# Seven columns of the second norm's modulation move from VectorE to GpSimd and ScalarE, inside the output projection's first half

## The chip, the cores and the metric

One NeuronCore of a Trainium2 chip runs the whole program. The metric is device time in microseconds (us) of one execution; before the change it is 1054.03 us, the median of 3 runs (1051.93 to 1054.62).

## The reference

One decoder layer for 256 tokens of width 2048, in float32. A conditioning vector c is turned into six vectors of 2048 numbers (shift, scale and gate for each of two sub-layers), by one product with a 2048 x 12288 matrix. What matters here is cut to these lines:

```python
c_act = jax.nn.silu(c)
mod = c_act @ w_mod[l] + b_mod[l]
sh1, sc1, g1, sh2, sc2, g2 = [m[:, None, :] for m in jnp.split(mod, 6, axis=-1)]
h = rmsnorm(x, attn_norm_g[l]) * (1.0 + sc1) + sh1
...                                   # input projection, two kinds of attention
mix = jnp.concatenate([o_a, o_b], axis=-1)
x = x + g1 * jnp.einsum('bsm,md->bsd', mix, w_out[l])
h = rmsnorm(x, mlp_norm_g[l]) * (1.0 + sc2) + sh2
u = jax.nn.relu(jnp.einsum('bsd,df->bsf', h, w_ff1[l]))
x = x + g2 * jnp.einsum('bsf,fd->bsd', u * u, w_ff2[l])
```

The second norm is the line with `sc2` and `sh2`: 16 blocks of 128 features each need one 128-wide column of `sc2` and one of `sh2`, 32 columns in all.

## The kernel before

Activations lie with features on the 128 partitions and the 256 tokens along the free axis; `x_sb` holds 16 such blocks. Large weights come in tiles of 128 x 2048 float32 (1 MB) by DMAs that SP issues. Weights of the two projections treated here are split into a high and a low part, 1024 columns at a time (`split`): ScalarE makes the high part (L191), VectorE subtracts it to get the low part (L192), and TensorE does three products for each 128 x 128 block (`mm3`, L197 to L199).

A modulation column (`mod_col`) is one 1 MB load (L161) and one VectorE instruction of 128 x 2048 that multiplies by the conditioning vector `c_bc`, sums along the row and adds the bias (L168), with a read of the accumulator behind it. The 32 columns of the second norm stand in a list, `modq`, in the order sc2, sh2, sc2, ...; `pump_mod(n)` takes the next n. Six are taken after the input projection (`NPRE`), behind the 16 columns of `g1`.

The output projection runs in two halves of the contraction. Half 0 takes the 8 heads' blocks of `mix[0]`, half 1 those of `mix[1]`. In each half, eight loads of `w_out` (dp = 0 to 7, L530) give two output tiles each (`out_tile`, d = 0 to 15): split, 24 matmuls, and a VectorE instruction that scales by `g1` and adds to `x_sb` (L536). The first two tiles of half 0 are put between the last units of attention; the other 14 follow it. In half 1 each tile's squares go into the second norm's sum (`SumSq`: ScalarE squares, GpSimd adds at L512), and `PB = (0, 1)` with `PBN = 8` takes one column of `modq` for each dp, eight in all. The other 18 are taken in the first part of the MLP's first product (the loop over kt after `pf`, called ff1a here, 48 matmuls for each kt): one for each kt from 1 on (`LEADK`), and more where the block kt itself would come without its pair. That makes two each at kt = 12, 13 and 14. `h2_tile(kt)` needs its two columns: GpSimd scales and multiplies (L693, L694), ScalarE adds the shift (L695), VectorE makes the low part (L696).

Buffers: weight tiles turn over three buffers (`NW`), columns over two (`NM`). The pool `at` holds attention's tiles and is closed at the beginning of half 1; in the room that it leaves stand the token-major tile `xt` and a pool `wide` with `WW = 4` further weight buffers and `WM = 2` further column buffers, until ff1a ends. Tile, the scheduling layer, sets each engine's order when the program is built, by the order of the source with some parts given priority, and puts in the waits; each engine's queue then runs in that order.

Of the kernel before, what the change touches and what calls it, by code (L numbers as in the profile page):

```python
# [9 lines left out]
F32 = mybir.dt.float32  # L10
F32R = mybir.dt.float32r
AF = mybir.ActivationFunctionType
ALU = mybir.AluOpType

P = 128
D = 2048
S = 256
KT = D // P
# [10 lines left out]
V_BMOD, V_GA, V_GM, V_GF, V_GQ, V_GKV = 0, 96, 112, 128, 144, 147  # L29
# [13 lines left out]
LEAD = 0  # L43
BORD = (1, 0)
BORD2 = (0, 1)
WW = 4
WM = 2
G2F = (1, 5)
G2E = (3, 4, 5, 6)
LEADK = (1, 1)  # L50
PBN = 8


@with_exitstack
def kernel(
# [21 lines left out]
    nc = tc.nc  # L77
    V, A, G, T = nc.vector, nc.scalar, nc.gpsimd, nc.tensor
# [9 lines left out]
    def bank(name):  # L88
        return ps.tile([P, 512], F32, tag="bank", name=name)

    def small(name, n=1, bufs=1):
        return keep.tile([P, n], F32, tag=name, name=name, bufs=bufs)
# [6 lines left out]
    vec = small("vec", 148)  # L99
# [18 lines left out]
    c_bc = keep.tile([P, D], F32, name="c_bc")  # L118
# [9 lines left out]
    b1 = small("b1", 32)  # L128
# [4 lines left out]
    wide = {}  # L133
# [171 lines left out]
    sc2, sh2 = {}, {}  # L305
    modq = [(p, i) for i in range(KT) for p in (4, 3)]

    def pump_mod(n):
        for _ in range(n):
            if modq:  # L310
                p, i = modq.pop(0)
                (sc2 if p == 4 else sh2)[i] = mod_col(p, i)
# [127 lines left out]
    def swa_values(u0, u1):  # L440

        u0.po.append(bank(f"po{u0.name}"))
        for kb in range(u0.b + 1):
            u0.value(kb)
            u1.value(kb)
        mix_out(u0.po[0], 4 * u0.half, u0.b)
# [79 lines left out]
    def out_tile(half, d):  # L526
        dp, d2 = divmod(d, 2)
        if d2 == 0:
            wo[half] = raw(f"wo{half}_{dp}")
            nc.sync.dma_start(wo[half], w_out[half, dp])  # L530
        wh, wl = split(wo[half], d2, f"wo{half}_{dp}")
        pd = bank(f"pd{half}_{d}")
        for k in range(8):
            o = k * P
            mm3(pd[:, 0:S], wh[:, o : o + P], wl[:, o : o + P], mix[half][:, k, :], k == 0, k == 7)
        V.scalar_tensor_tensor(out=x_sb[:, d, :], in0=pd[:, 0:S], scalar=g1[d], in1=x_sb[:, d, :],  # L536
                               op0=ALU.mult, op1=ALU.add)

    with tc.high_priority():
# [92 lines left out]
        for n, u in enumerate(units):  # L632
# [14 lines left out]
            elif n % 2:  # L647
                swa_values(units[n - 1], u)

    def to_tokens(dp):  # L650
        pt = bank(f"xt{dp}")
        for t in range(2):
            for i in range(2):
                T.transpose(out=pt[:, (2 * t + i) * P : (2 * t + i + 1) * P],
                            in_=x_sb[:, 2 * dp + i, t * P : (t + 1) * P], identity=ident)
        A.activation(out=xt[:, :, 2 * dp * P : (2 * dp + 2) * P], in_=pt.rearrange("p (t c) -> p t c", t=2),
                     func=AF.Copy)

    for half in range(2):
        if half:  # L660
            ap_stack.close()
            late = ctx.enter_context(tc.tile_pool(name="late", bufs=1))
            xt = late.tile([P, 2, D], F32, name="xt")
            wide_stack = ExitStack()
            wide.update(pool=wide_stack.enter_context(tc.tile_pool(name="wide", bufs=1)), w=WW, m=WM)
        for dp in range(8):
            for d2 in range(2):
                d = 2 * dp + d2
                if half or dp:
                    out_tile(half, d)  # L670
                if half:
                    ss2.add(d)
                if half == 0 or dp < PBN:
                    pump_mod((PA, PB)[half][d2])
            if half and dp:
                to_tokens(dp - 1)

    with tc.high_priority():
        r2 = ss2.rstd()
    to_tokens(7)  # L680


# [289 lines left out]
```

## Time and profile before

| | before |
|---|---|
| median of 3 runs | 1054.03 us |
| profiled execution | 1053.02 us |
| its span, first to last instruction | 1051.2 us |
| TensorE busy | 1008.8 us (96%) |
| VectorE busy | 723.2 us (69%) |
| ScalarE busy | 487.4 us (46%) |
| GpSimd busy | 101.2 us (10%) |
| mean DMA rate | 267 GB/s |

The profiled execution spends 1.8 us outside its span. The views are read by stretches of time: attention ends near 222 us, half 0 of the output projection ends near 262, half 1 near 310, and ff1a runs from 317 to about 418. The names PE, DVE, ACT, POOL and SP in the rows are TensorE, VectorE, ScalarE, GpSimd and the queue that issues the DMAs; the time from the start of one record to the start of the next is the rate at which an engine works, since records overlap a little.

### The profile page before, as it was taken

Reading aid. Unit: us, or ns where it says so; the run is one execution under the profiler, and the core shown is the slowest. Engines: PE = TensorE matmul, PEld = TensorE weight load, DVE = VectorE, ACT = ScalarE, POOL = GpSimd, SP = SyncE. Lnnn points to the kernel's source line nnn. Section 1 sums busy time; section 2 is a strip of 40 time slices with the busy share of each in tenths; the row PEclk is TensorE's granted clock in tenths of the full one; section 3 lists DMA queues with packets and bytes.
Section 4 is the critical chain, followed back from the end, with each engine's and each line's share of the span. In section 5 each row is a group of like instructions: output and inputs, shape, how many; then the busy total and the mean of one; then the engine's idle time right before and its main releaser. Section 6 shows DMA issues by size and latency. Waiting matters only on the chain.

```text
span 1051.2 us, 14181 instructions
## 1 busy us (share of the span) xinstructions
PE 1008.8 (96%) x5582; PEld 866.6 (82%) x5582; DVE 723.2 (69%) x923; ACT 487.4 (46%) x824; POOL 101.2 (10%) x78
## 2 busy tenths in 40 slices
PE   6999989999987998999999999999999999999996
PEld 5777766799977998888888888888888888888885
DVE  5676769999987887897774555545555566554673
ACT  2000087743553443884444665334566543455461
POOL 0000014000448325000000000000000000000110
PEclk9999999999998999999999999999999999999998
DMA  8999986889996875889887655555555555555551
GB/s 328 422 420 420 410 333 240 307 327 398 419 387 255 308 258 228 319 323 339 312 304 257 224 177 189 195 200 200 172 189 196 177 191 196 201 185 179 197 200 80
DMA packets 44259, 280.24 MB, mean 267 GB/s; under 512 B 6880, under 2 KB 9120, under 8 KB 13088
## 3 DMA queue, kind: packets, MB, share of 16 engines
q1 hardware_dynamic: 44192, 279.34, 71.1%
q8 instruction: 43, 0.70, 0.3%
q14 instruction: 24, 0.20, 0.1%
HBM read 277.19 MB, written 2.13 MB: 266 GB/s over the span
## 4 chain that ended last, share of the span: by engine, by line
PE 73%; DVE 10%; DMA 8%; ACT 4%; POOL 2%; issue 2%; SPq 0%; ACTq 0%; DVEq 0%; POOLq 0%
PE pu L203 17%; PE pd L814 11%; PE pd L812 11%; PE pd L813 11%; PE pu L204 9%; DMA wm<-in_w_mod 7%; DVE wm L168 5%; PE pj L271 5%; PE pf L199 2%; PE pf L198 2%; PE pf L197 2%; POOL xn L693 1%; DVE wo_lo L192 1%; DMA wo<-in_w_out 1%; ACT ssa L349 1%
## 5 line engine op out<-in xcount | busy, mean ns | idle before, releaser
L192 DVE TENSOR_TENSOR wf_lo<-wf,wf_hi 128x1024 fp32r<-128x1024 f32 x250 | 308.5, 1239 | 222.9 <-ACT wf_hi L191 222.3
L191 ACT ACTIVATE wf_hi<-wf 128x1024 fp32r<-128x1024 f32 x250 | 263.7, 1056 | 238.0 <-PE pd L814 169.1
L203 PE MATMUL pu<-h,wf_hi 128*128 128x512 f32 x768 | 270.2, 397 | 0.0
L204 PE MATMUL pu<-h,wf_lo 128*128 128x256 f32 x768 | 215.5, 281 | 0.0
L812 PE MATMUL pd<-wf_hi,u 128*128 128x512 f32 x488 | 189.9, 389 | 0.0
L814 PE MATMUL pd<-wf_hi,u 128*128 128x512 f32 x488 | 189.9, 389 | 0.0
L813 PE MATMUL pd<-wf_lo,u 128*128 128x512 f32 x488 | 189.9, 389 | 0.0
L203 PEld LDWEIGHTS pu<-h,wf_hi 128*128 128x128 f32 x768 | 144.1, 188 | 34.7
L168 DVE CUSTOM_DVE_ANT_0 wm<-wm,c_bc,vec 128x2048 f32<-128x2048 f32 x64 | 151.5, 2367 | 14.2 <-DMA wm<-in_w_mod 14.1
L204 PEld LDWEIGHTS pu<-h,wf_lo 128*128 128x128 f32 x768 | 145.1, 189 | 0.1
L271 PE MATMUL pj<-h,wi 128*128 128x256 f32 (+1 forms) x480 | 113.1, 392 | 7.8 <-ACT h L257 7.8
L271 PEld LDWEIGHTS pj<-h,wi 128*128 128x128 f32 (+1 forms) x480 | 89.0, 191 | 31.4 <-ACT h L257 12.7
L814 PEld LDWEIGHTS pd<-wf_hi,u 128*128 128x128 f32 x488 | 91.6, 188 | 19.0
L812 PEld LDWEIGHTS pd<-wf_hi,u 128*128 128x128 f32 x488 | 91.6, 188 | 19.0
L813 PEld LDWEIGHTS pd<-wf_lo,u 128*128 128x128 f32 x488 | 91.6, 188 | 19.0
L168 DVE CUSTOM_DVE_ANT_0 wm<-wm,c_bc,b 128x2048 f32<-128x2048 f32 x32 | 75.9, 2371 | 31.3 <-DMA wm<-in_w_mod 31.2
L199 PE MATMUL pf<-h,wf_lo 128*128 128x256 f32 x256 | 74.4, 294 | 5.9 <-DVE wf_lo L192 5.9
L197 PE MATMUL pf<-h,wf_hi 128*128 128x256 f32 x256 | 74.0, 293 | 6.1 <-ACT h L695 5.0
L197 PE MATMUL pd<-mix,wo_hi 128*128 128x256 f32 x256 | 73.9, 289 | 1.3 <-ACT wo_hi L191 1.3
L198 PE MATMUL pf<-h,wf_hi 128*128 128x256 f32 x256 | 74.4, 292 | 0.0
L199 PE MATMUL pd<-mix,wo_lo 128*128 128x256 f32 x256 | 72.5, 284 | 0.0
L198 PE MATMUL pd<-mix,wo_hi 128*128 128x256 f32 x256 | 72.5, 283 | 0.0
(195 smaller groups left out, 1095.1 us busy)
## 6 DMA issues: line engine op xcount, KB each, us to landing
wm<-in_w_mod SPq DMA_DIRECT2D x96, 1024.0 KB, 9.2
wf<-in_w_ff SPq DMA_DIRECT2D x64, 1024.0 KB, 4.8
wf<-in_w_ff1b SPq DMA_DIRECT2D x48, 1024.0 KB, 4.9
wo<-in_w_out SPq DMA_DIRECT2D x16, 1024.0 KB, 12.1
wf<-in_w_ff1a SPq DMA_DIRECT2D x16, 1024.0 KB, 8.5
wi<-in_w_in SPq DMA_DIRECT2D x15, 928.0 KB, 13.9
x_sb<-in_xT SPq DMA_DIRECT2D x4, 512.0 KB, 5.5
bias<-g_dr SPq DMA_DIRECT2D x2, 1024.0 KB, 12.5
```

The source lines that it names most:

```text
L168: V.tensor_tensor_reduce(out=t, in0=t, in1=c_bc, scale=1.0, scalar=init, op0=ALU.mult, op1=ALU.add, accum_out=col)
L191: A.activation(out=hi, in_=src, func=AF.Copy)
L192: V.tensor_tensor(out=lo, in0=src, in1=hi.bitcast(F32), op=ALU.subtract)
L197: T.matmul(out, lhsT=wh, rhs=a[:, 0:S], start=start, stop=False, **kw)
L198: T.matmul(out, lhsT=wh, rhs=a[:, S : 2 * S], start=False, stop=False, **kw)
L199: T.matmul(out, lhsT=wl, rhs=a[:, 0:S], start=False, stop=stop, **kw)
L203: T.matmul(out, lhsT=wh, rhs=a, start=start, stop=False)
L204: T.matmul(out[:, 0:S], lhsT=wl, rhs=a[:, 0:S], start=False, stop=stop)
L271: T.matmul(proj(j)[: e - j * P, :], lhsT=w[:, j * P : e], rhs=h, start=(kt == 0 and j % 2 == 0), stop=(kt == KT - 1), skip_group_check=True)
L812: T.matmul(pd[t], lhsT=uh, rhs=wh[:, o : o + 512], start=(f == 0), stop=False)
L813: T.matmul(pd[t], lhsT=uh, rhs=wl[:, o : o + 512], start=False, stop=False)
L814: T.matmul(pd[t], lhsT=ul, rhs=wh[:, o : o + 512], start=False, stop=(f == KT - 1))
```

## The change

`pool_mod` does one column without VectorE's long instruction: the load goes to a buffer of its own (tag `widep`, 2 buffers), GpSimd multiplies by `c_bc` in place (128 x 2048), ScalarE copies the result in place and sums it into a column, and VectorE adds the bias (128 x 1). It is called seven times, ahead of the two tiles of dp = 1 to 7 in half 0. For that, attention's pool is closed and `xt` and `wide` are opened at the beginning of half 0 instead of half 1. The further weight buffers go from 4 to 3 and the further column buffers from 2 to 1, which is the room of the two `widep` buffers. `PBN` goes from 8 to 4, so four columns are taken in half 1 instead of eight. By the same count 15 instead of 18 are left for ff1a: one for each kt from 1 to 15.

```diff
-WW = 4
-WM = 2
+WW = 3
+WM = 1
 G2F = (1, 5)
 G2E = (3, 4, 5, 6)
 LEADK = (1, 1)
-PBN = 8
+PBN = 4
...
+    def pool_mod():
+
+        p, i = modq.pop(0)
+        t = wide["pool"].tile([P, 2048], F32, tag="widep", name=f"wp{p}_{i}", bufs=2)
+        nc.sync.dma_start(t, w_mod[p * KT + i])
+        G.tensor_tensor(out=t, in0=t, in1=c_bc, op=ALU.mult)
+        col = small(f"mod{p}_{i}")
+        A.activation(out=t, in_=t, func=AF.Copy, accum_out=col)
+        init = b1[:, 16 + i : 17 + i] if p == 4 else vec[:, V_BMOD + p * KT + i : V_BMOD + p * KT + i + 1]
+        V.tensor_tensor(out=col, in0=col, in1=init, op=ALU.add)
+        (sc2 if p == 4 else sh2)[i] = col
+
...
     for half in range(2):
-        if half:
+        if half == 0:
             ap_stack.close()
             late = ctx.enter_context(tc.tile_pool(name="late", bufs=1))
             xt = late.tile([P, 2, D], F32, name="xt")
             wide_stack = ExitStack()
             wide.update(pool=wide_stack.enter_context(tc.tile_pool(name="wide", bufs=1)), w=WW, m=WM)
         for dp in range(8):
+            if half == 0 and dp:
+                pool_mod()
             for d2 in range(2):
```

## Rows read from the trace of the kernel before

**Rows 1.** Windows by stage: length, busy time (instructions) by engine, PE clock, DMA share, GB/s.
```profile
222.00:262.00 40.00, 38.70 (x315) 37.80 (x315) 38.00 (x46) 13.10 (x13) 0.00 (x0) 1.00 0.97 383
262.00:310.00 48.00, 47.04 (x391) 46.73 (x391) 45.66 (x49) 23.33 (x35) 22.98 (x14) 1.00 1.00 408
317.30:343.00 25.70, 22.25 (x146) 21.38 (x147) 18.65 (x22) 8.86 (x14) 20.12 (x14) 0.84 0.66 252
343.00:397.00 54.00, 54.00 (x452) 54.00 (x451) 47.46 (x48) 20.77 (x22) 19.03 (x10) 1.00 0.77 287
```

**Rows 2.** VectorE's groups from 222 to 310: count, busy us, mean ns, idle before.
```profile
L192 DVE TENSOR_TENSOR wo_lo<-wo,wo_hi 128x1024 fp32r<-128x1024 f32 x27 | 34.7, 1300 | 1.8 <-ACT wo_hi L191 1.6
L168 DVE CUSTOM_DVE_ANT_0 wm<-wm,c_bc,b 128x2048 f32<-128x2048 f32 x8 | 19.0, 2370 | 0.1
L536 DVE SCALAR_TENSOR_TENSOR x_sb<-pd,mod,x_sb 128x256 f32<-128x256 f32 x28 | 13.3, 476 | 1.9 <-PE pd L199 1.9
L168 DVE DVE_READ_ACCUMULATOR2_ANT mod<- 128x1 f32 x16 | 1.3, 79 | 0.0
```

**Rows 3.** Windows at the end of ff1a, and one from its middle (columns as in Rows 1).
```profile
397.00:403.00 6.00, 5.70 (x48) 5.50 (x47) 5.00 (x6) 2.41 (x3) 2.30 (x2) 1.00 0.98 399
403.00:409.00 6.00, 4.71 (x38) 4.30 (x36) 4.83 (x5) 2.40 (x3) 3.15 (x2) 1.00 0.91 381
409.00:415.00 6.00, 4.02 (x21) 4.02 (x22) 5.44 (x7) 0.00 (x0) 4.99 (x2) 0.72 0.01 4
349.00:355.00 6.00, 6.00 (x52) 6.00 (x51) 4.36 (x6) 2.71 (x4) 3.21 (x2) 1.00 0.91 358
```

**Rows 4.** GpSimd's two-input products, undisturbed, 256 and 512 wide: start, duration.
```profile
321.74 0.74 POOL L694 TENSOR_TENSOR xn<-xn,r_y 128x256 f32<-128x256 f32 x1
1021.86 1.29 POOL L848 TENSOR_TENSOR xt<-x_sb,gf_row 128x512 f32<-128x512 f32 x1 [18.48 <-DVE x_sb L846]
```

**Rows 5.** Timeline: GpSimd and VectorE at work at the same time.
```profile
978.14 3.52 POOL L848 TENSOR_TENSOR xt<-x_sb,gf_row 128x512 f32<-128x512 f32 x2 [563.08 <-DVE x_sb L846]
978.52 4.22 DVE L192 TENSOR_TENSOR wf_lo<-wf,wf_hi 128x1024 fp32r<-128x1024 f32 x2
...
999.84 3.53 POOL L848 TENSOR_TENSOR xt<-x_sb,gf_row 128x512 f32<-128x512 f32 x2 [18.18 <-DVE x_sb L846]
1002.15 1.25 DVE L852 TENSOR_TENSOR sbase<-ssum 128x2 f32<-128x2 f32 x1
...
303.98 2.19 POOL L512 TENSOR_TENSOR sqa<-sqa,sqr 128x256 f32<-128x256 f32 x1 [2.13 <-ACT sqr L510]
303.25 2.34 DVE L168 CUSTOM_DVE_ANT_0 wm<-wm,c_bc,vec 128x2048 f32<-128x2048 f32 x1
305.51 0.47 DVE L536 SCALAR_TENSOR_TENSOR x_sb<-pd,mod,x_sb 128x256 f32<-128x256 f32 x1
```

**Rows 6.** Groups of ScalarE: a copy of 1024, a square of 256, an accumulator read.
```profile
L191 ACT ACTIVATE wo_hi<-wo 128x1024 fp32r<-128x1024 f32 x32 | 33.5, 1053 | 34.0 <-PE pd L198 22.1 <-DMA wo<-in_w_out 11.9
L510 ACT ACTIVATE sqr<-x_sb 128x256 f32<-128x256 f32 x15 | 6.3, 417 | 13.7 <-DVE x_sb L536 13.7
L847 ACT ACTIVATION_READ_ACCUMULATOR pd<-x_sb 128x1 f32 x8 | 1.5, 186 | 0.0
```

**Rows 7.** Timeline of a load, attention's last matmul, a split; then landing times.
```profile
201.58 0.33 SPq L530 DMA_DIRECT2D wo<-in_w_out  x1
...
222.30 0.38 PE L486 MATMUL pob<-pTb,vB 128*128 128x128 f32 x2
225.22 1.06 ACT L191 ACTIVATE wo_hi<-wo 128x1024 fp32r<-128x1024 f32 x1 [1.90 <-PE pd L198]
...
DMA to landing us min/median/max: 5.9/12.1/18.7
```

**Rows 8.** What TensorE waited for from 195 to 310, the two projection rows.
```profile
PE pd L197 <- ACT wo_hi L191: 1.3, 3, 0.5
PE pr L515 <- POOL sqa L512: 1.0, 1, 1.0
```

**Rows 9.** Window of the highest DMA rate in the output projection (columns as in Rows 1).
```profile
250.00:275.00 25.00, 24.18 (x199) 23.68 (x198) 22.53 (x28) 11.37 (x14) 4.45 (x3) 1.00 1.01 423
```

## The prediction

> **What bounds the kernel now.** I read the windows by stage first. In half 0 of the output projection after attention (222 to 262 us) and in half 1 (262 to 310) TensorE is busy for 38.7 of 40 and 47.0 of 48 us, and VectorE for 38.0 and 45.7 [rows 1]: two engines are full at once. The list of waits says which of them sets the pace: TensorE waited 1.3 us in all for a split weight tile and 1.0 us for the sum of squares [rows 8]. So TensorE is the bound there, at 8.1 matmuls a us (391 in 48 us), and VectorE keeps up with hardly anything to spare. No work taken from VectorE can shorten these two stretches by more than about 2 us; work added to its path can lengthen them one for one.
>
> Where TensorE does lose time is ff1a. Its middle is saturated, 52 matmuls in 6 us [rows 3] and 452 in 54 us [rows 1]. Its end, where three kt carry two columns each, is not: 48, 38 and 21 matmuls in three windows of 6 us [rows 3], which is 4 + 14 + 31 = 49 fewer than full, or 49 x 6 / 52 = 5.6 us lost. The granted clock fell to 0.72 in the last of these, after TensorE had stood; that is inside the 5.6. Its start (317.3 to 343) has 146 matmuls where 54 us in the middle have 452, so 215 would fit: 69 short, 8.2 us [rows 1]. There TensorE starts cold after the norm, and GpSimd is busy or waiting for 20.1 of 25.7 us.
>
> **What the change takes away.** Seven VectorE columns of 2.37 + 0.08 = 2.45 us [rows 2], 17.2 us in all: four from half 1 (9.8 us, where TensorE is the bound, so worth nothing by themselves) and three from kt = 12, 13, 14. With one column for each kt, the end looks like the middle, where TensorE never stood. I take the whole 5.6 us (between 3 and 5.6; not above, since there is nothing more to win there). The start of ff1a keeps one column for each kt; four fewer columns in half 1 may let the next ones run earlier. Nearest rows: 8.2 us is lost there in all, mostly to the chain behind the norm, which is untouched. I take 0, with ends of -4 and +2.
>
> **What the products cost on GpSimd.** An undisturbed two-input instruction takes 0.74 us at 256 and 1.29 us at 512 [rows 4]: 0.55 us for each further 256, so 2048 takes 1.29 + 6 x 0.55 = 4.6 us. Seven are 32.2 us, on an engine that has nothing to do from 222 to 262 [rows 1].
>
> **That cover is not free, and this decides.** Two GpSimd products of 512 beside two VectorE subtractions took 3.52 and 4.22 us [rows 5]. One after the other: product until 979.4 (1.29), subtraction until 980.5, product until 981.7, subtraction until 982.7, which is exactly when both records end. An addition of 128 x 2 took 1.25 us beside such a product and ended with it (1002.15 + 1.25 = 1003.40; 999.84 + 3.53 = 1003.37). So an instruction of VectorE with both inputs in SBUF and a GpSimd product shut each other out for their whole length. L168 and L192 are of that kind. L536, which takes one input from PSUM, is not: beside a GpSimd addition that ran once L168 had ended at 305.6, it took its usual 0.47 us [rows 2, 5]. Moving a column thus takes 2.45 us off the shared path and puts 4.6 us on it.
>
> No instruction wider than 512 is in the trace on GpSimd. The Trainium skill (SBUF — State Buffer, section Who interferes with whom) says that such a pair holds the shared read path for the whole instruction and that the later one blocks fully, whatever the size. By it each product is one block of 4.6 us; rows to 512 agree, and no row here shows 2048. If instead a long product let VectorE in, the sum would be the rival "no block" below. The Trainium skill (GPSIMD Engine Reference, section Performance versus the Vector engine) gives 4.5 us for such an instruction of 2048; the term would be 0.7 us smaller by it.
>
> **The budget of half 0.** VectorE's 38.0 us plus 32.2 us of products, less the thirteen L536 that can run beside them (13 x 0.476 = 6.2), is 64.0 us in a stretch of 40: 24.0 too many [rows 1, 2]. Some products can slip into half 1. There VectorE has 45.7 - 9.8 = 35.9 us; GpSimd's own thirteen additions add 13 x 0.74 = 9.6, and fifteen L536 beside them take off 7.1: 38.4 of 48, so 9.6 us, two products, find room. That leaves **14.4 us** [rows 1, 2, 4], by which the weight splits come late and TensorE stands. Ends: 24 if none slips (the two `widep` buffers let a product lag by no more than two), and 2 or less if the products go in pieces or start in attention.
>
> **Waits behind the products.** ScalarE's copy with sum: (1053 - 417) / 768 = 0.83 ns an element, so 1.05 + 0.85 + 0.19 = 2.1 us, 14.7 us for seven, on an engine busy for 13.1 of 40 [rows 1, 6]. Its time is hidden; its place need not be. ScalarE and VectorE run in order: if the copy stands ahead of a split and its product is late, L191 waits, and TensorE behind it; so does VectorE behind the small bias addition. Three split buffers cover about two tiles, 5.7 us. I take 0 beyond the port term, since a VectorE that waits leaves the path to GpSimd; up to +15 if the order is unlucky.
>
> **The room.** Before, the fourth `w_out` tile was issued at 201.58 and split at 225.22 [rows 7]. After, it and the products' loads go into attention's room, which is read until 222.3 at least. The fastest landing was 5.9 us, the median 12.1 [rows 7], so it lands between 229 and 235, 4 to 9 us after its old split. TensorE still has a tile in hand then, and the first product is no earlier either. I take +2 (0 to +8). The third load on, `pool_mod`'s issue also waits for a `widep` buffer, with later `w_out` loads queued behind it on SP; their three more buffers cover that. In half 1 and ff1a one weight buffer and one column buffer fewer cost nothing as long as ff1a runs at 287 GB/s [rows 1].
>
> **DMA.** Half 0 moves 383 GB/s [rows 1]; the highest rate shown is 423 [rows 9]. Spare: 40 GB/s x 40 us = 1.6 MB, against 7.3 MB more. The rest displaces loads ahead for half 1, which needs four fewer. I take 0; if nothing gives way it is 5.7 / 0.423 = 13.6 us, beside the port term and not on top of it.
>
> **Sum**, against the profiled execution: 1053.0 + 14.4 + 2 - 5.6 = 1063.8 us. The median of the runs is 1.0 us above that execution: **1065 us**.
>
> **Rivals.**
> - *No block* (faster): a 2048-wide product gives way in between, or falls into VectorE's gaps. For it: no row at that width. Against it: every pair in [rows 5]. Then half 0 keeps its time and ff1a's end is won, with up to 2 us at its start: 1054 - 5.6 - 1 = 1047 us. Chance 0.14.
> - *The products slip* (no change): they start late, four or more fall into half 1 and into the norm's gap at 310, and the port term is 5 or 6 us, as large as the gain. That is also the case in which the change does not put the work where it says. 1051 to 1057 us. Against it: only two buffers. Chance 0.14.
> - *Queues stand* (slower still): ScalarE's copies and SP's buffer waits stop splits and loads for whole products. It decides once a product is later than the two tiles in hand. Half 0 then goes in steps of product, copy and split, 4.6 + 2.1 + 2 x 1.3 = 9.3 us for each dp where 5.7 would do: 7 x 3.6 = 25 us, 1054 + 25 + 5 - 5.6 = 1078 us, to 1088. Chance 0.20.
> - The forecast, 1057.2 to 1074 us: 0.52.
>
> The range reaches from 1049 to 1083: some 0.10 lies below it and 0.07 above. About 0.3%, 3.2 us, is what a measurement here can tell from no change: faster 0.14, within 0.14, slower 0.72.
>
> **What would show it.** Right: products of 4.6 us or more on GpSimd between 228 and 275; L168 or L192 of 3 to 7 us beside them and L536 at 0.48; TensorE waiting for `wo_lo` or `wo_hi` in half 0, its end near 275 to 280 and not 262; the end of ff1a at 52 matmuls in 6 us. Wrong: L192 at 1.2 us beside a running product, or half 0 no longer than before. If ScalarE's L191 waits for GpSimd, it is the third rival.

## The result, and the profile after

The changed kernel takes 1095.31 us (1093.48 to 1097.85, 4 runs) where the kernel before took 1052.98 beside it (1050.36 to 1054.62): a ratio of 1.040, 95% interval 1.038 to 1.042, some 42 us slower. The forecast of 1065 had the sign, and its range ended 12 us too low.

Where the 42 us lie is read by stages first. From the start of the first output tile's L536 to that of the 16th, which is half 0, it was 51.6 us before and is 90.5 after; from the 16th to the 32nd (half 1) 49.0 and 49.1; from the first matmul of `pf` to the first of the MLP's next product (ff1a) 106.1 and 106.7. So half 0 has taken 39 us more, and nothing has been won anywhere. The profiled execution is 43.7 us longer; of what half 0 leaves of that, 1.1 us lie between half 1 and `pf` and 2.8 behind ff1a, and they were not followed up.

Windows of the changed kernel: stand, rest of half 0, half 1, and three parts of ff1a (length, busy us and instructions of TensorE, its weight loads, VectorE, ScalarE, GpSimd, then granted clock, DMA share, GB/s).

```profile
226.60:257.60 31.00, 1.08 (x10) 0.88 (x8) 15.58 (x18) 5.89 (x6) 15.05 (x4) 0.55 0.88 349
257.60:303.00 45.40, 39.68 (x277) 38.85 (x278) 33.74 (x38) 22.51 (x25) 19.18 (x4) 0.82 0.79 318
303.00:352.00 49.00, 47.51 (x388) 46.25 (x386) 39.59 (x42) 23.45 (x37) 19.45 (x14) 1.00 0.83 308
...
358.50:384.00 25.50, 21.05 (x142) 20.24 (x141) 13.69 (x18) 7.69 (x12) 18.90 (x16) 0.84 0.51 195
384.00:438.00 54.00, 50.81 (x405) 50.20 (x406) 45.98 (x47) 21.54 (x25) 17.05 (x12) 0.97 0.81 312
438.00:459.00 21.00, 21.00 (x177) 21.00 (x176) 16.44 (x16) 7.79 (x8) 0.00 (x0) 1.00 0.48 179
```

Against [rows 1, 3]: TensorE did ten matmuls in 31 us; half 1 is what it was; the end of ff1a is full (177 matmuls in 21 us, which is 51 in 6 us), yet its middle has 405 matmuls in 54 us where it had 452. The 47 missing there are, but for two, the 49 won at the end.

The list of waits of the changed kernel, TensorE, 195 to 400 (us in all, times, longest), against [rows 8]:

```profile
PE pd L197 <- ACT wo_hi L191: 31.2, 2, 31.0
PE pd L199 <- DVE wo_lo L192: 4.4, 2, 2.7
```

One stand of 31 us, for the fourth weight tile's high part. The timeline of the changed kernel shows what stood ahead of that split, on SP and on ScalarE (start, duration, what was waited for):

```profile
222.94 0.33 SPq L654 DMA_DIRECT2D wp<-in_w_mod  x1
227.99 4.15 SPq L161 DMA_DIRECT2D wm<-in_w_mod  x2
232.19 0.42 SPq L654 DMA_DIRECT2D wp<-in_w_mod  x1
238.79 3.66 SPq L161 DMA_DIRECT2D wm<-in_w_mod  x2
242.54 0.38 SPq L654 DMA_DIRECT2D wp<-in_w_mod  x1
242.98 0.50 SPq L530 DMA_DIRECT2D wo<-in_w_out  x1
...
236.64 1.91 ACT L657 ACTIVATE wp<-wp 128x2048 f32<-128x2048 f32 x1 [14.31 <-POOL wp L655]
246.76 1.91 ACT L657 ACTIVATE wp<-wp 128x2048 f32<-128x2048 f32 x1 [8.12 <-POOL wp L655]
255.72 1.91 ACT L657 ACTIVATE wp<-wp 128x2048 f32<-128x2048 f32 x1 [6.96 <-POOL wp L655]
257.63 1.99 ACT L191 ACTIVATE wo_hi<-wo 128x1024 fp32r<-128x1024 f32 x2
```

The load of that tile, the first in attention's old room, left SP at 242.98 where its forerunner left at 201.58 [rows 7]: three product loads and four column loads went ahead of it. On ScalarE three sums, each behind its product, stood ahead of the split. This looks like the third rival. The experiments show that it is mostly where the time appears, and not what makes it.

The products, and VectorE beside them, by the same timeline:

```profile
232.11 4.49 POOL L655 TENSOR_TENSOR wp<-wp,c_bc 128x2048 f32<-128x2048 f32 x1 [50.52 <-DVE mod L168]
275.03 5.51 POOL L655 TENSOR_TENSOR wp<-wp,c_bc 128x2048 f32<-128x2048 f32 x1 [0.33 <-DMA wp<-in_w_mod]
...
257.76 3.06 DVE L659 TENSOR_TENSOR mod<-mod,b 128x1 f32<-128x1 f32 x1 [6.41 <-ACT wp L657]
275.98 0.48 DVE L536 SCALAR_TENSOR_TENSOR x_sb<-pd,mod,x_sb 128x256 f32<-128x256 f32 x1
276.37 6.38 DVE L192 TENSOR_TENSOR wo_lo<-wo,wo_hi 128x1024 fp32r<-128x1024 f32 x2
```

The shortest product takes 4.49 us (4.6 was worked out from [rows 4]). Two subtractions that take 2.6 us by [rows 2] took 6.38 beside one, an addition of 128 x 1 took 3.06, and L536 kept its 0.48. The exclusion read from [rows 5] at 512 holds at 2048, and the rival "no block" is out.

### The profile page after: what moved, and what is told of

Read it like the earlier page. It is cut to its first block, busy times and chain, and to the rows that moved or that the text cites. A ratio compares the mean times of both kernels' runs of the same rounds, so it can differ in the third digit from the quotient of the medians.

```text
span 1095.0 us, 14188 instructions
## 1 busy us (share of the span) xinstructions
PE 1015.8 (93%) x5582; PEld 872.2 (80%) x5582; DVE 718.2 (66%) x916; ACT 501.2 (46%) x838; POOL 118.2 (11%) x85
## 4 chain that ended last, share of the span: by engine, by line
PE 74%; DVE 9%; DMA 9%; ACT 4%; POOL 2%; issue 2%; SPq 0%; DVEq 0%; ACTq 0%; POOLq 0%
PE pu L203 16%; PE pd L828 11%; PE pd L826 11%; PE pd L827 11%; PE pu L204 8%; DMA wm<-in_w_mod 7%; DVE wm L168 5%; PE pj L271 4%; PE pf L199 2%; PE pf L197 2%; PE pf L198 2%; PE pd L199 2%; PE pd L197 2%; PE pd L198 2%; DVE wo_lo L192 1%
## 5 line engine op out<-in xcount | busy, mean ns | idle before, releaser
L192 DVE TENSOR_TENSOR wf_lo<-wf,wf_hi 128x1024 fp32r<-128x1024 f32 x250 | 308.1, 1236 | 249.9 <-ACT wf_hi L191 249.6
L168 DVE CUSTOM_DVE_ANT_0 wm<-wm,c_bc,vec 128x2048 f32<-128x2048 f32 x61 | 146.3, 2399 | 7.6 <-DMA wm<-in_w_mod 7.3
L197 PE MATMUL pd<-mix,wo_hi 128*128 128x256 f32 x256 | 76.3, 298 | 31.2 <-ACT wo_hi L191 31.2
L168 DVE CUSTOM_DVE_ANT_0 wm<-wm,c_bc,b 128x2048 f32<-128x2048 f32 x28 | 69.2, 2472 | 39.1 <-DMA wm<-in_w_mod 39.1
L197 PE MATMUL pf<-h,wf_hi 128*128 128x256 f32 x256 | 74.2, 295 | 9.1 <-ACT h L709 6.1
L199 PE MATMUL pd<-mix,wo_lo 128*128 128x256 f32 x256 | 75.5, 296 | 4.4 <-DVE wo_lo L192 4.4
L862 POOL TENSOR_TENSOR xt<-x_sb,gf_row 128x512 f32<-128x512 f32 x6 | 10.5, 1771 | 627.3 <-DVE x_sb L860 627.3
L197 PEld LDWEIGHTS pd<-mix,wo_hi 128*128 128x128 f32 x256 | 51.8, 202 | 31.7 <-ACT wo_hi L191 31.7
```

Source lines behind the costliest of these rows:

```text
L168: V.tensor_tensor_reduce(out=t, in0=t, in1=c_bc, scale=1.0, scalar=init, op0=ALU.mult, op1=ALU.add, accum_out=col)
L192: V.tensor_tensor(out=lo, in0=src, in1=hi.bitcast(F32), op=ALU.subtract)
L197: T.matmul(out, lhsT=wh, rhs=a[:, 0:S], start=start, stop=False, **kw)
L199: T.matmul(out, lhsT=wl, rhs=a[:, 0:S], start=False, stop=stop, **kw)
```

## The experiments

All times against the kernel before, run on the same chip. Stages as above: half 0, half 1, ff1a, each from the profiled execution (before: 51.6, 49.0, 106.1; changed: 90.5, 49.1, 106.7). The kernel before lay between 1052.0 and 1053.1 us in the rounds, so a difference between runs of two rounds is good to about 1 us.

| run | us (range) | before beside it | ratio, 95% | half 0 | half 1 | ff1a |
|---|---|---|---|---|---|---|
| e_room | 1062.68 (1061.36–1063.92) | 1052.0 | 1.007–1.012 | 62.4 | 49.2 | 101.9 |
| e_noprod | 1081.34 (1079.2–1082.65) | 1052.0 | 1.024–1.029 | 76.8 | 49.1 | 107.3 |
| e_ring | 1094.45 (1092.63–1095.34) | 1052.0 | 1.037–1.042 | 88.2 | 50.2 | 106.4 |
| e_queue | 1093.4 (1092.6–1096.71) | 1052.0 | 1.037–1.042 | 81.2 | 56.6 | 105.2 |
| e_queue_noprod | 1076.97 (1075.09–1079.69) | 1052.85 | 1.021–1.025 | 68.0 | 52.6 | 105.6 |
| e_ring_room | 1052.36 (1049.82–1057.7) | 1052.85 | 0.998–1.002 | 51.4 | 49.0 | 106.2 |
| e_dummy | 1084.74 (1082.55–1088.62) | 1052.85 | 1.028–1.033 | 76.2 | 58.1 | 103.6 |
| e_spread | 1057.2 (1054.29–1057.72) | 1052.85 | 1.002–1.005 | 51.2 | 49.0 | 109.0 |
| e_gone | 1054.62 (1053.16–1057.21) | 1053.12 | 1.001–1.003 | 51.3 | 48.4 | 106.4 |
| e_dummy_gone | 1091.8 (1090.29–1092.76) | 1053.12 | 1.035–1.038 | 76.4 | 59.0 | 106.3 |
| e_ring_noprod | 1075.84 (1072.31–1077.21) | 1053.12 | 1.019–1.023 | 71.4 | 48.4 | 106.4 |
| e_ring_small | 1058.42 (1055.74–1064.49) | 1053.12 | 1.004–1.008 | 54.3 | 50.7 | 106.4 |
| e_hold | 1049.4 (1046.87–1050.88) | 1052.35 | 0.995–0.998 | 54.4 | 49.0 | 100.8 |
| e_gone_hold | 1043.27 (1040.93–1044.94) | 1052.35 | 0.989–0.993 | 51.6 | 48.4 | 94.5 |
| e_small_prod | 1073.28 (1070.79–1074.73) | 1052.35 | 1.017–1.021 | 72.2 | 50.2 | 103.3 |
| e_hold_spread | 1044.82 (1041.42–1046.01) | 1052.35 | 0.988–0.994 | 53.3 | 49.0 | 95.3 |

### The room alone, and the products taken out

e_room is the kernel before with the early opening and `WW = 3`, `WM = 1`, and no `pool_mod`. e_noprod is the changed kernel with the product taken out:

```diff
-        G.tensor_tensor(out=t, in0=t, in1=c_bc, op=ALU.mult)
```

> Only the room changes: attention's pool is closed and the further weight buffers open at the beginning of half 0 (three further weight buffers, one further column buffer), and no column goes to GpSimd; eight columns are taken in half 1 as before. Theory P (the read path that VectorE and GpSimd share costs most of the 42 us): without a product nothing is lost, 1051 to 1057 us. Theory Q (the order of SP's and ScalarE's queues costs most of it): the fourth w_out tile now waits for attention's end, behind two columns' loads, and lands some 6 us after its old split; TensorE stands for 5 to 8 us, 1057 to 1063 us.

> The changed kernel without GpSimd's seven products (they are left out: ScalarE sums the plain weights), with all loads, buffers, sums and additions as they are. P: the shared path is free again, and the time falls to 1050 to 1062 us. Q: the fourth w_out tile is still issued behind three of the new loads and six columns on SP, about 242 us, and its split still stands behind three sums; only the waits for products go, 5 to 12 us of the 31 us in which TensorE stood: 1080 to 1090 us.

The early opening alone costs 10.7 us, and half 0 is 10.9 longer (ff1a was 4.2 shorter in it and the rest as much longer; this was not followed up). Three tiles of half 0, the fourth to the sixth, are loaded into attention's room, and ScalarE stood before the first split of each. Its timeline in e_room:

```profile
230.89 2.00 ACT L191 ACTIVATE wo_hi<-wo 128x1024 fp32r<-128x1024 f32 x2 [10.21 <-DVE mod L168]
240.78 2.01 ACT L191 ACTIVATE wo_hi<-wo 128x1024 fp32r<-128x1024 f32 x2 [7.88 <-DMA wo<-in_w_out]
248.58 2.01 ACT L191 ACTIVATE wo_hi<-wo 128x1024 fp32r<-128x1024 f32 x2 [5.80 <-DMA wo<-in_w_out]
```

The first of these waits is put down to VectorE, but that tile's load left SP at 220.94 and landed at 230.79, 0.1 us ahead of its split. Without the products 29 of the 42 us stay. So the shared path is not most of it, and 18 us beyond the room have another cause, taken at first to be the queues.

### Mending the room and the queues

e_ring takes the further weight buffers only from half 1 on, so half 0 turns over its three old ones:

```diff
-            wide.update(pool=..., w=WW, m=WM)
+            wide.update(pool=..., w=0, m=WM)
+        else:
+            wide["w"] = WW
```

e_queue issues the `w_out` loads two pairs ahead, each product's load behind them, and each sum one pair later, behind the splits.

> The changed kernel, but the further weight buffers are used from half 1 on only, so that w_out tiles four and five of half 0 are loaded into the three old buffers as before; products, sums and their buffers stay as they are. P: the products and VectorE's work are the same, 1088 to 1097 us. Q: TensorE goes on for four more tiles (11.5 us) and then stands for the sixth w_out tile, whose load and split now stand behind four sums: 1079 to 1087 us.

> The changed kernel with its seven products, sums and buffers, but in another order: each w_out tile of half 0 is asked for two pairs of tiles ahead, a product's load is issued behind the w_out load before it, and its sum is put one pair of tiles later on ScalarE, behind that pair's splits. P: the products take the shared path as before, 1085 to 1095 us. Q: TensorE no longer stands for w_out, and what remains is the path's own price, at most the 14 us of the forecast: 1055 to 1070 us.

Neither gains more than 2 us: 1094.45 and 1093.4. In e_ring the stand moved to a later tile and was 23.3 us long; in e_queue it fell into several. e_queue does not mend everything: it keeps the buffers in attention's room, and SP stood 39.1 us at product loads until a sum freed a `widep` buffer, with later `w_out` loads behind them. Two runs go on from there:

> e_queue without GpSimd's products (the seven columns are sums of the plain weights; the multiplication by the conditioning vector is left out for them). Loads, buffers, ScalarE's sums and the mended order of the queues stay. Theory O (of the 29 us that the kernel without products is over the kernel before, the 18 us beyond the room's 10.7 come from the order in which SP and ScalarE take the new work): 1058 to 1066 us, TensorE's waits for wo_hi near 9 us in all. Theory A (they come from the amount: seven more megabytes through half 0's buffers, whatever the order): 1074 to 1083 us, waits for wo_hi of 20 us or more. The difference from e_queue (1093.4) is then the price of the products: 27 to 35 by O, 10 to 19 by A; the port budget says 14.4, at most 24.

> The room opens at half 0 as in e_room, without any new column there, but the further weight buffers are taken only from half 1 on, so half 0 turns over its three old buffers. Theory L (the 10.7 us of e_room are the fourth w_out tile, whose buffer in attention's room opens late): 1050 to 1056 us, TensorE's waits for wo_hi under 3 us in all. Rival W (they come from anything else that the early opening brings, as one further weight buffer and one further column buffer less, or the token-major tile at another place): 1060 to 1065 us.

e_ring_room is back at the time before (1052.36), so the room's 10.7 us are the late buffers of tiles four to six and nothing else. e_queue_noprod, with the order mended as far as above and the products gone, still takes 1077, the time of theory A (the amount), though TensorE waited 17.1 us for `wo_hi` where A asked for 20 or more. Its late buffers can account for 10.7 of its 24 us, so it does not part amount from order by itself; the next two runs do better.

### The bytes

e_ring_noprod is e_ring without products. e_ring_small is the same with one sixteenth of the bytes; its sums read `c_bc`, which is as wide, since most of the tile is not loaded, and still wait for the load:

```diff
-        nc.sync.dma_start(t, w_mod[p * KT + i])
+        nc.sync.dma_start(t[:, 0:128], w_mod[p * KT + i][:, 0:128])
-        A.activation(out=t, in_=t, func=AF.Copy, accum_out=col)
+        A.activation(out=t, in_=c_bc, func=AF.Copy, accum_out=col)
```

> e_ring without GpSimd's products (left out: the multiplication of the seven columns by the conditioning vector). The late weight buffer is gone, the shared path is free; seven loads and seven sums of ScalarE stay in half 0. If room, loads and products add up (10.7 + 15 to 18 + 14), this is 1052.5 + 15 to 18 = 1067 to 1071 us. If the three overlap (e_ring gained nothing over the changed kernel), 1074 to 1082 us.

> e_ring_noprod with loads of 128 x 128 in place of 128 x 2048 (one sixteenth of the bytes), and with ScalarE's sums as long as before (they read the conditioning vector's tile, and wait for the load as before): the same instructions, waits and order of the queues, without the seven megabytes. Theory B (half 0's DMA is near its limit, so the bytes cost): 1052 to 1057 us, at least 10 below e_ring_noprod. Theory H (it is the order: SP stands at a load whose buffer is not free, ScalarE at a sum, with w_out's loads and splits behind): within 4 us of e_ring_noprod.

The bytes cost 1075.8 - 1058.4 = 17.4 us. A window of e_ring_noprod and then the same of e_ring_small, 240 to 262:

```profile
240.00:262.00 22.00, 7.16 (x44) 6.67 (x43) 10.83 (x17) 10.66 (x11) 0.00 (x0) 0.69 0.99 376
```

```profile
240.00:262.00 22.00, 17.39 (x129) 16.76 (x128) 17.21 (x28) 14.90 (x16) 0.00 (x0) 0.92 0.92 341
```

In the first the DMA engines are busy all the time (0.99) and TensorE has 44 matmuls, in the second 129. The bytes left out are 7 x 15/16 x 1.049 = 6.9 MB, which is 395 GB/s over 17.4 us: close to the 383 that half 0 moved before [rows 1]. The whole of half 0, in the kernel before and then in e_ring_noprod:

```profile
209.67:261.25 51.58, 49.34 (x401) 47.84 (x400) 48.89 (x59) 19.41 (x23) 0.00 (x0) 1.00 0.93 362
209.37:280.80 71.43, 52.43 (x399) 50.77 (x398) 50.90 (x68) 33.05 (x37) 0.00 (x0) 0.88 0.94 363
```

That is 18.7 MB and some 26 MB at the same rate: the products' loads came on top of all that half 0 moved before, and half 0 had no time in hand for them. e_ring_small also shortens the waiting for these loads to land (ScalarE's sums waited 18.8 us for them in e_ring_noprod and 8.8 in e_ring_small), so its 17.4 us are the transfer and the waits for it together. More `widep` buffers, which could part the two, were not tried.

### The products

e_dummy is the kernel before with seven products whose result nobody uses, on a tile of attention that is dead by then, each tied behind an output tile by a copy of one column:

```diff
+    def lone(dp):
+        t = vB.rearrange("p b d -> p (b d)")
+        G.tensor_copy(out=t[:, 0:1], in_=x_sb[:, 2 * dp - 1, 0:1])
+        G.tensor_tensor(out=t, in0=t, in1=c_bc, op=ALU.mult)
```

> The kernel before with seven lone GpSimd products of 128 x 2048 in half 0, in place on a tile of attention that is dead by then; no load, no sum, nobody waits for their results. Each begins after the output tile of the dp ahead of it. Theory P (the shared read path, by the budget of the prediction): 1060 to 1077 us, 1066 the likeliest; VectorE's L168 or L192 of 4 to 7 us beside each product. Theory N (the path is worth nothing by itself; the products cost only through those who wait for them): 1051 to 1055 us.

It costs 32 us, more than the budget's 24. The window of e_dummy from 222 to 262, and then VectorE's groups in it:

```profile
222.00:262.00 40.00, 27.43 (x187) 26.62 (x186) 40.00 (x25) 7.41 (x7) 29.52 (x9) 0.84 0.56 206
```

```profile
L192 DVE TENSOR_TENSOR wo_lo<-wo,wo_hi 128x1024 fp32r<-128x1024 f32 x8 | 25.8, 3236 | 0.0
L168 DVE CUSTOM_DVE_ANT_0 wm<-wm,c_bc,vec 128x2048 f32<-128x2048 f32 x2 | 9.1, 4526 | 0.0
...
L536 DVE SCALAR_TENSOR_TENSOR x_sb<-pd,mod,x_sb 128x256 f32<-128x256 f32 x8 | 3.7, 475 | 0.0
```

VectorE is never idle, with L192 at 3.24 us against 1.30 in [rows 2] and L536 as it was. Half 0 is 24.6 us longer, close to the budget's 24.0. Half 1 is 9.1 longer, at its head. The list of waits of e_dummy, ScalarE, 270 to 310:

```profile
ACT wo_hi L191 <- DMA wo<-in_w_out: 17.1, 1, 17.1
```

VectorE frees the load buffers, so while it was held up the DMA engines idled (share 0.56), and half 1 began with no tile loaded. Two further runs set the products beside what the change takes away, and beside its sums and order:

> e_gone with the seven lone GpSimd products of e_dummy in half 0: the change without its loads, its sums and its early room. The prediction's port budget: 24 us too many in half 0, of which half 1, with four columns fewer, takes up 9.6, so 14.4 us over e_gone. If half 1 gives nothing back, as in e_dummy (whose half 1 has no room), 23 to 32 us over e_gone. If the path is worth nothing without those who wait, 0 to 3 us over e_gone.

> e_ring_small with the seven GpSimd products (both inputs the conditioning vector, of the same size and place in the queue, so the values of the seven columns are not the reference's): products and sums, without the seven megabytes. If the products cost here what they cost alone (32 us in e_dummy): 1058.4 + 32 = 1090 us, and the bytes on top are worth only 4 (e_ring has 1094.5). If they cost what they cost beside the bytes (e_ring less e_ring_noprod, 18.6): 1077 us, and each cause is worth its 17 to 19 in any company.

e_dummy_gone is 37 us over e_gone, more than any of the expectations: four fewer columns in half 1 give nothing back. In e_small_prod seven products placed as in the change cost 1073.3 - 1058.4 = 14.9 us, less than either expectation. TensorE's wait there is VectorE's, by the list of e_small_prod, 200 to 440, and then one product of the same run:

```profile
PE pd L199 <- DVE wo_lo L192: 16.4, 4, 6.4
```

```profile
241.82 3.95 POOL L655 TENSOR_TENSOR wp<-c_bc 128x2048 f32<-128x2048 f32 x1 [0.59 <-DMA wp<-in_w_mod]
```

With `c_bc` as both inputs a product took 3.95 us here and 3.59 at the shortest, where the shortest of the change took 4.49. So 14.9 us is rather too low for the change's own products. The other runs that take the products out of a kernel with all its bytes give 14.0 (changed kernel less e_noprod), 16.4 (e_queue less e_queue_noprod) and 18.6 (e_ring less e_ring_noprod).

### The gain that did not come

e_spread moves the three doubled columns to kt = 5, 8 and 11:

```diff
-        pump_mod(LEAD if kt == 0 else LEADK[kt % 2])
+        pump_mod(LEAD if kt == 0 else LEADK[kt % 2] + (kt in (5, 8, 11)))
```

e_gone leaves the seven columns out, with `PBN = 4`.

> The kernel before, with the three columns that double up at kt = 12, 13, 14 of ff1a moved to kt = 5, 8 and 11 (VectorE does them there too); the number of columns by each place else is unchanged. Theory E (the 5.6 us at the end of ff1a are lost to the doubling, and the middle has room for one more column every third kt): 1045 to 1049 us against 1052. Theory V (VectorE is what ff1a runs by as a whole, so that a column taken early gives back in the middle what the end wins): 1050 to 1054 us, with fewer than 452 matmuls in the 54 us before the end.

> The kernel before without the seven columns (their loads and VectorE instructions are left out; their values are taken from the first column), four fewer in half 1 and one for each kt in ff1a: all that the change takes away and nothing that it adds. Theory G (the prediction's gain: the end of ff1a gives 5.6 us): 1045 to 1049 us against 1052.5, 409 to 415 as full as the middle. Theory F (ff1a is bound as a whole by what it loads and by VectorE, so the three columns fewer are given back ahead of its end, or more is won since seven megabytes are not loaded at all): outside of that, 1050 or more, or under 1044.

Neither is faster than before. All that the change takes away is worth nothing, even when nothing is put in its place. Windows of e_gone in the first third and at the end of ff1a:

```profile
343.00:361.00 18.00, 14.79 (x107) 14.18 (x106) 12.77 (x15) 6.07 (x8) 11.14 (x5) 0.91 0.72 253
...
409.00:415.00 6.00, 6.00 (x52) 6.00 (x51) 6.00 (x6) 2.15 (x3) 0.00 (x0) 1.00 0.46 169
```

The end is full, and the first third has 107 matmuls where the kernel before had 152:

```profile
343.00:361.00 18.00, 18.00 (x152) 18.00 (x151) 16.36 (x17) 7.49 (x8) 7.38 (x3) 1.00 0.76 289
```

Timeline of e_gone there, GpSimd, ScalarE and TensorE:

```profile
342.74 2.96 POOL L697 TENSOR_SCALAR xn<-x_sb,a 128x256 f32<-128x256 f32 x1
345.79 0.72 POOL L698 TENSOR_TENSOR xn<-xn,r_y 128x256 f32<-128x256 f32 x1
346.55 0.51 ACT L699 ACTIVATE h<-xn,mod 128x256 fp32r<-128x256 f32 x1 [3.24 <-POOL xn L698]
346.96 1.99 ACT L191 ACTIVATE wf_hi<-wf 128x1024 fp32r<-128x1024 f32 x2
348.05 0.39 PE L197 MATMUL pf<-h,wf_hi 128*128 128x256 f32 x1 [2.27 <-ACT wf_hi L191]
```

ScalarE waits with `h` of a later kt for GpSimd, GpSimd is held up (2.96 us for an instruction that takes 0.93 elsewhere), the splits of the kt at hand stand behind, and TensorE behind them. In the kernel before, ScalarE's queue has `h` up to four kt ahead of the first split of a kt; counted in the same way it is six in e_gone and seven in the changed kernel. That this costs the time is a theory until the order is changed. e_hold does it in the kernel before, e_gone_hold in e_gone:

```diff
-        A.activation(out=h2[kt][:, 0:S], in_=xn, func=AF.Identity, bias=sh2[kt])
+        with tc.issue_after(last_of["w", 0]) if kt > 1 else ExitStack():
+            A.activation(out=h2[kt][:, 0:S], in_=xn, func=AF.Identity, bias=sh2[kt])
```

where `last_of["w", 0]` is the first split of the kt before.

> The kernel before, with one thing else in ff1a: ScalarE's activation h (L695) of each kt from 2 on stands behind the first weight split of the kt before it, where it had run up to four kt ahead of the splits. Theory H (the first third of ff1a is slow because the splits stand in ScalarE's queue behind activations that wait for GpSimd): 1045 to 1050 us against 1053. Rival C (the splits wait for something else there, VectorE's subtractions or the clock that TensorE starts with): 1051 to 1056 us.

> e_gone (the seven columns left out) with the same order in ScalarE's queue. Theory H: the 5.6 us that the end of ff1a gives are no longer lost at its first third, so this is 4 to 6 us below e_hold and 343 to 361 has about 150 matmuls and not 107. Rival C: 1052 to 1056 us, within 2 us of e_hold.

> e_hold with the three columns of kt = 12 to 14 taken at kt = 5, 8 and 11 as in e_spread. Theory H: the end of ff1a is full and the middle keeps its pace, 3 to 5 us below e_hold. Rival D (in the middle the loads, two tiles of 1 MB for each kt and a third at 5, 8 and 11, are what e_spread lost to): as e_spread, 1054 to 1058 us, or e_hold + 3.

The theory holds. A window of e_gone_hold in the first third (343 to 361 has 152 matmuls as well), and then two of e_hold_spread:

```profile
340.00:358.00 18.00, 18.00 (x152) 18.00 (x151) 17.96 (x19) 7.56 (x9) 14.21 (x7) 1.00 0.99 390
```

```profile
343.00:361.00 18.00, 18.00 (x153) 18.00 (x152) 18.00 (x20) 7.71 (x10) 12.70 (x7) 1.00 0.88 339
...
409.00:415.00 6.00, 6.00 (x52) 6.00 (x51) 3.44 (x5) 4.08 (x10) 0.00 (x0) 1.00 0.47 167
```

With the splits ahead, taking the columns away is worth 1049.4 - 1043.3 = 6.1 us, and only moving them 4.6. **e_hold_spread is the version that beats both kernels**: 1044.82 us, 0.988 to 0.994 of the kernel before, all 32 columns on VectorE. It needs nothing of GpSimd. Its ff1a is 10.7 us shorter; half 0 was 1.7 us longer in this execution and 2.8 in e_hold's, though neither touches a line there. The granted clock was 0.83 in 252 to 262 of both, against 1.00 before; why is open.

## Why the prediction was right or wrong

Most of the signs that the prediction named came as written: the products, VectorE's instructions beside them, L536 and the end of ff1a. But half 0 ended at 300 us and not at 275 to 280.

The five runs that add the change up in one order: e_gone 1054.6, with sums, waits and small loads 1058.4 (e_ring_small), with products 1073.3 (e_small_prod), with the bytes 1094.5 (e_ring), with the further weight buffers early 1095.3. With the bytes ahead of the products it is 1058.4, 1075.8, 1094.5. So in the change's company the products are worth 14 to 19 us (14.0 with e_noprod), the bytes 17.4 to 21.2 (the upper end leans on the shorter products of e_small_prod), sums, small loads and their waits 3.8, the room 0.9, which is within the noise between rounds, and taking the columns away wins nothing (1.5 us slower). Products and bytes add up almost in full, though neither engine is full for the whole of half 0. The changed kernel there:

```profile
209.89:300.35 90.46, 54.19 (x398) 52.92 (x398) 62.79 (x70) 32.93 (x37) 34.23 (x7) 0.75 0.83 327
```

VectorE is busy for 62.8 of 90.5 us and the DMA share is 0.83. What keeps the two costs from overlapping was not tested; the two `widep` buffers, for which SP stood 24.4 us, are the first suspect.

- **DMA: "I take 0".** The step that failed most: 17 to 21 us, above even its bound of 13.6. The rows for it were in hand: a share of 0.97 in half 0 [rows 1], and ScalarE waiting 11.9 us for `w_out` loads there [rows 6]. The prediction let "the rest" of the 7.3 MB displace loads for half 1. Nothing gave way: half 0 of e_ring_noprod moved some 7.3 MB more at the same rate, and even the 1.6 MB that the bound took for spare room cost their time (395 GB/s for all of the bytes). The four loads that half 1 is spared come later, in a stretch that TensorE bounds (49.0 us with them, 48.4 without).
- **The end of ff1a: "I take the whole 5.6 us".** The end did fill, as the prediction's last part foresaw. The step "the start of ff1a, I take 0" failed: the chain behind the norm was called untouched, but with more columns ready more `h` stand ahead of the splits (seven kt where it was four), and 47 matmuls went there. The net is nothing; with ScalarE's order mended it is 6.1.
- **The port: 14.4.** The mechanism is right, and the size lies at the low end of the 14 to 19 us measured; the 24.0 for half 0 if nothing slips is close to the 24.6 of e_dummy. That 14.4 comes so near is in part luck, for the step between, that two products find room in half 1, was not seen: in e_small_prod half 0 is 17.9 us longer than in e_ring_small, half 1 only 0.5 shorter, and 3.1 came back in ff1a; e_dummy_gone shows half 1 giving nothing back. What brought 24 down to 18 was not isolated; VectorE was busy for 35.0 of 40 us in e_ring_small where the budget had 38.0, and the products of e_small_prod are shorter.
- **The room: +2.** By itself it is 10.7. In e_room the fourth tile landed at 230.79, inside the predicted 229 to 235, so that step held. What failed is the step from there to the cost. The split at 225.22 [rows 7] is the second of that tile, the eighth of half 0 by ScalarE's timeline before; its first came earlier:

```profile
220.85 1.06 ACT L191 ACTIVATE wo_hi<-wo 128x1024 fp32r<-128x1024 f32 x1 [1.87 <-PE pd L198]
```

So by the predicted landing the tile is 8 to 14 us late and not 4 to 9, and two more tiles stood in the same room: the "three more buffers" that were to cover the waits were the late ones. In the changed kernel the load left only at 242.98, 20 us after attention, since SP takes loads in order and others waited for their own buffers ahead of it. Beside bytes and products the late room costs 0.9 or nothing; that the same loads are late anyway is the likely reason, not a tested one.

- **Waits behind the products: 0.** They stand in the trace, 31 us of them, as the third rival said. But the order by itself is worth little: with small loads and no products the longest stand is 4.0 us (e_ring_small), with the products added TensorE waits for VectorE's `wo_lo` and no longer for ScalarE (e_small_prod), and e_queue's other order gained 1.9 us. The third rival had the place, not the cause, and its time, 1078 to 1088 us, ended 7 us short. An order mended together with the room was not run.

## What to carry to other kernels

Ask of each stage what its DMA share is before moving a load into it: here, at 0.97, each megabyte cost 2.5 us, its full transfer time, however idle the engine that was to use it. The longest wait in a trace says where lateness shows, not what makes it: the stand of 31 us moved, split and stayed while its supposed cause was taken away. And before pricing a relief, leave the relieved work out: here that run gave nothing, and pointed to an order in another engine's queue that was worth 3 us alone and 7.5 with the columns moved.

## What the runs showed of the hardware

- A whole 2048-wide product on GpSimd and a VectorE instruction with two SBUF inputs exclude each other as the narrow ones did: in e_dummy an L168 that began 2.1 us into a product took 6.71 us, where it takes 2.34 alone. The Trainium skill (SBUF — State Buffer, section Who interferes with whom) says so of the whole instruction; these traces agree. The row of e_dummy, VectorE:

```profile
249.78 6.71 DVE L168 CUSTOM_DVE_ANT_0 wm<-wm,c_bc,vec 128x2048 f32<-128x2048 f32 x1
```

- GpSimd's `TENSOR_SCALAR` of 128 x 256, which has one tensor in SBUF, is shut out too. GpSimd and VectorE of e_gone, timeline:

```profile
322.12 0.75 POOL L698 TENSOR_TENSOR xn<-xn,r_y 128x256 f32<-128x256 f32 x1
322.85 4.03 POOL L697 TENSOR_SCALAR xn<-x_sb,a 128x256 f32<-128x256 f32 x1
327.67 0.93 POOL L697 TENSOR_SCALAR xn<-x_sb,a 128x256 f32<-128x256 f32 x1
...
322.18 2.84 DVE L168 CUSTOM_DVE_ANT_0 wm<-wm,c_bc,vec 128x2048 f32<-128x2048 f32 x1
324.95 1.22 DVE L192 TENSOR_TENSOR wf_lo<-wf,wf_hi 128x1024 fp32r<-128x1024 f32 x1
```

It took 4.03 us, from the end of the product before to 0.7 us after L192's, against 0.93 five microseconds later.

- A stand costs more than itself. In the 31 us the granted clock fell to 0.50, which is 1.2 GHz, the lower of TensorE's two levels. The changed kernel, windows of 10 us:

```profile
250.00:260.00 10.00, 1.12 (x3) 0.83 (x4) 3.59 (x3) 3.90 (x4) 8.47 (x2) 0.50 0.77 294
260.00:270.00 10.00, 8.22 (x48) 7.93 (x47) 5.95 (x8) 5.82 (x7) 6.58 (x3) 0.63 0.72 289
270.00:280.00 10.00, 9.00 (x75) 8.76 (x73) 7.57 (x8) 6.11 (x7) 9.67 (x2) 1.00 0.87 359
```

The window behind it has 48 matmuls at a clock of 0.63, the next 75 at 1.00.
